# ACT and VectorE in a written order from the last head's output to the output projection, and the last row's scaling shared by both

## The chip, the core and the metric

The kernel runs on one core of one Trainium2 chip. A core has five engines with queues of their own: TensorE (PE, with its weight loads PEld), VectorE (DVE), ScalarE (ACT), GpSimd (POOL) and SyncE (SP), which here only issues transfers. Each takes its own instructions in order and waits on semaphores for the others. The metric is the device time of one execution in microseconds (us), the median of the runs.

## The reference

```python
h = rms_norm(x, norm_mix_g); u = h @ w_in            # 1024 tokens x 1024 -> 3328 columns
u_pool, q_raw, f_raw, i_raw, g_raw = split(u)        # 256 + 4 x 768 columns
y_pool = pool_mixer(u_pool)                          # trailing means over 2/4/8/16, a map per group
y_hgrn = hgrn2_mixer(q_raw, f_raw, i_raw, g_raw)     # 6 heads, state 128x128, chunkwise;
                                                     # per-head RMSNorm, swish gate on the output
x = x + concat([y_pool, y_hgrn]) @ w_out
x = x + square(relu(rms_norm(x) @ w_up)) @ w_down    # 4096 hidden channels
return rms_norm(x, final_norm_g)
```

All arrays are float32 and batch and depth are 1.

## The kernel before

**Products.** Every float32 operand of a large product is split into a rounded part `hi` and a remainder `lo`: `split` (L119) writes `hi` with an ACT cast (L121) and `lo` with a DVE subtraction that reads `hi` (L122). `mm3` (L124) then does three matmuls, hi*hi (L127), hi*lo (L128) and lo*hi (L129). A product with a weight block can so begin when the block's `whi` is there, and its third matmul needs `wlo` as well.

**The mixing stage** (the first 370 us) is a loop over six heads `hd` (L721). For each head the chain `hgrn` (L393) runs in stages named near, middle, far, keys, updates and output; beside it the generator `beside(hd)` (L603) makes the dense products that the next head needs (`q`, the forget input `f`, the gate `g`, for two heads the values `v` or the pooling input `u`). Between the stages PE takes as many steps of that dense work as the table `LAGS` says; one step is one k-tile, three matmuls. `load_w` (L159) brings a weight block from HBM into one of two `raw` buffers and splits it into a ring of four `whi` and four `wlo` buffers. A dense product `dense_T` (L346) sums eight steps into a PSUM bank, and DVE scales the bank into its tile (L355). `q` and `g` go through a sigmoid on ACT (L361) and a product on DVE (L362), `f` through three ACT operations (L367 to L369). For each head `hgrn` begins with DVE products (`d0`, `d1`, L398 to L401), `deepen` (L526) multiplies `q`, `k` and the decays level by level, and ACT copies pairs of blocks (`kq`, L410 and L411) for PE. The stage updates carries the state over seven chunks on DVE (`st`, L502 and L504). The stage output forms `po` on PE (L513 and L515), takes its squares on ACT (L518), the scale with DVE and POOL (`rstd_of`, L131), and the scaled output `on` on DVE (L520). `mixed` (L537) transposes `on` on PE (`pto`) and gates it into the `mix` tile (L544), one head later.

**The handover.** After the last head the eight `mix` tiles are split into `mT` (`mix_split`, L748), four blocks of the left half of `w_out` are loaded and split (`wo`), and PE computes the first two row tiles `ps_o` with k-tiles in the order of `MIX_ORDER` (2, 3, 4, 5, 6, 0, 1, 7). The transposes of the last head stand behind the first three k-tiles.

**What sets the order.** PE's order is written out through the whole mixing stage (`tc.manual_schedule` with PE alone, L720). The order of DVE, ACT and POOL there is the scheduler's: it may put an instruction ahead of what stands before it in the text. DVE and ACT are in a written order in the prologue, in the first group of the MLP (L989) and in the last two products.

**The end.** The last row tile's right half is computed in two pieces of 256 columns (L1237). Their sums of squares are taken on ACT (L1128), POOL makes the row scale (L1143), then DVE scales the left 512 columns (L1147, sent by SP) and ACT the right 512 (L1151, sent from ACT's own queue).

## Time and profile before

| what | value |
| --- | --- |
| three runs | 1071.29 to 1071.64 us, median 1071.42 us |
| the profiled execution | 1071.58 us, of which the span from first to last instruction is 1069.8 us |
| mean granted TensorE clock | 0.999 |
| PE busy | 1060.4 us (99%) |
| DVE busy | 741.7 us (69%) |
| ACT busy | 447.7 us (42%) |
| POOL busy | 77.3 us (7%) |

A row of the timeline gives start, duration, engine, line, operation, output and input, and in brackets how long the engine stood idle before and what ended that. A row of windows gives busy time and instruction count of PE, PEld, DVE, ACT and POOL in a stretch, then the granted clock, the DMA share and GB/s. The span's start is 0. Matmuls overlap: one lasts 0.39 us in the rows, while in a dense stretch the next starts some 0.23 us after it.

### The profile page before, as it was taken

How to read it: one execution, taken by the hardware profiler on the slowest of the kernel's cores; microseconds unless marked ns; L12 is line 12 of the kernel's file. 1: busy time of each engine (PE TensorE's matmuls, PEld its weight loads, DVE VectorE, ACT ScalarE, POOL GpSimd, SP SyncE). 2: the span in 40 equal slices, each digit the busy share in tenths (PEclk: the TensorE clock that was granted, in tenths of full speed). 3: DMA queues.
4: the chain of work that ended last, by engine and by line, in shares of the span. 5: the costliest groups of instructions: out<-in, count | busy, mean ns of one | idle time of the engine just before them, and what ended most of it. 6: DMA issues, size and time to landing. Idle time of an engine off the chain costs nothing.

```text
span 1069.8 us, 14595 instructions
## 1 busy us (share of the span) xinstructions
PE 1060.4 (99%) x5930; PEld 889.6 (83%) x5930; DVE 741.7 (69%) x928; ACT 447.7 (42%) x722; POOL 77.3 (7%) x126
## 2 busy tenths in 40 slices
PE   9999999999999999999999999999999999999997
PEld 8988889988888788888888888888888888888886
DVE  5377676166587924798856865876979878777775
ACT  5856545344444723463223223323435242423334
POOL 0001000001010111101101100100100000000001
PEclk9999999999999999999999999999999999999999
DMA  9521011031001633135435534428983344253104
GB/s 315 169 60 55 17 30 40 3 97 41 21 1 41 202 134 117 70 108 177 167 109 189 185 101 156 177 98 318 389 335 119 114 162 170 105 204 150 40 1 157
DMA packets 70515, 137.56 MB, mean 129 GB/s; under 512 B 5040, under 2 KB 44080, under 8 KB 66864
## 3 DMA queue, kind: packets, MB, share of 16 engines
q1 hardware_dynamic: 59808, 100.98, 27.8%
q0 software_dynamic: 9344, 33.56, 8.0%
q10 hardware_dynamic: 1296, 2.10, 0.5%
q8 instruction: 46, 0.75, 0.3%
q14 instruction: 21, 0.17, 0.1%
HBM read 98.87 MB, written 37.75 MB: 128 GB/s over the span
## 4 chain that ended last, share of the span: by engine, by line
PE 95%; DVE 3%; DMA 0%; issue 0%; POOL 0%; ACT 0%; SPq 0%; ACTq 0%; POOLq 0%
PE ps_ua L128 5%; PE ps_ua L127 5%; PE ps_ua L129 5%; PE ps_dx L129 5%; PE ps_dx L127 5%; PE ps_dx L128 5%; PE ps_v L283 3%; PE ps_dy L129 3%; PE ps_uc L128 3%; PE ps_dy L127 3%; PE ps_uc L127 3%; PE ps_uc L129 3%; PE ps_dy L128 3%; PE ps_o L129 2%; PE ps_o L128 2%; PE ps_o L127 2%
## 5 line engine op out<-in xcount | busy, mean ns | idle before, releaser
L121 ACT CAST wdop<-raw_wd 128x2048 fp32r<-128x2048 f32 x28 | 53.5, 1912 | 154.3 <-PE ps_dy L129 50.2
L127 PE MATMUL ps_ua<-h2op,whi_wu 128*128 128x512 f32 x256 | 99.7, 389 | 0.0
L129 PE MATMUL ps_ua<-h2op,wlo_wu 128*128 128x512 f32 x256 | 99.6, 389 | 0.0
L128 PE MATMUL ps_ua<-h2op,whi_wu 128*128 128x512 f32 x256 | 99.6, 389 | 0.0
L127 PE MATMUL ps_dx<-wdop,hop 128*128 128x512 f32 x252 | 98.0, 389 | 0.0
L128 PE MATMUL ps_dx<-wdop,hop 128*128 128x512 f32 x252 | 98.0, 389 | 0.0
L129 PE MATMUL ps_dx<-wdop,hop 128*128 128x512 f32 x252 | 98.0, 389 | 0.0
L122 DVE TENSOR_TENSOR wdop<-raw_wd,wdop 128x2048 fp32r<-128x2048 f32 x28 | 64.1, 2289 | 27.9 <-ACT wdop L121 27.9
L121 ACT CAST hop<-hraw 128x2048 fp32r<-128x2048 f32 x28 | 53.4, 1909 | 33.6 <-DMA hraw<-hid 21.0
L122 DVE TENSOR_TENSOR hop<-hraw,hop 128x2048 fp32r<-128x2048 f32 x28 | 63.9, 2283 | 2.2 <-ACT hop L121 2.2
L121 ACT CAST whi_wu<-wsum 128x1024 fp32r<-128x1024 f32 x22 | 23.2, 1053 | 93.6 <-DVE wsum L795 38.7
L122 DVE TENSOR_TENSOR wlo_wu<-raw_wu,whi_wu 128x1024 fp32r<-128x1024 f32 x23 | 28.0, 1221 | 47.6 <-ACT whi_wu L121 47.6
L798 DVE TENSOR_TENSOR x<-ps_dx,x 128x512 f32<-128x512 f32 x64 | 43.9, 687 | 18.7 <-PE ps_dx L129 18.7
L127 PEld LDWEIGHTS ps_ua<-h2op,whi_wu 128*128 128x128 f32 x256 | 48.1, 188 | 10.0
L129 PEld LDWEIGHTS ps_ua<-h2op,wlo_wu 128*128 128x128 f32 x256 | 48.0, 188 | 10.0
L128 PEld LDWEIGHTS ps_ua<-h2op,whi_wu 128*128 128x128 f32 x256 | 48.1, 188 | 9.9
L128 PEld LDWEIGHTS ps_dx<-wdop,hop 128*128 128x128 f32 x252 | 47.3, 188 | 9.9
L129 PEld LDWEIGHTS ps_dx<-wdop,hop 128*128 128x128 f32 x252 | 47.3, 188 | 9.8
L127 PEld LDWEIGHTS ps_dx<-wdop,hop 128*128 128x128 f32 x252 | 47.3, 188 | 9.8
L1031 POOL DMA_DIRECT2D hid<-hid x56 | 29.8, 532 | 283.6 <-DVE hid L1028 216.5
L127 PE MATMUL ps_uc<-h2op,whi_wu 128*128 128x512 f32 x128 | 49.8, 389 | 0.0
L128 PE MATMUL ps_uc<-h2op,whi_wu 128*128 128x512 f32 x128 | 49.8, 389 | 0.0
(280 smaller groups left out, 2706.4 us busy)
## 6 DMA issues: line engine op xcount, KB each, us to landing
hid<-hid POOLq DMA_DIRECT2D x56, 512.0 KB, 3.2
hraw<-hid SPq DMA_DIRECT2D x28, 1024.0 KB, 4.8
raw_wu<-in_w_up_dram SPq DMA_DIRECT2D x32, 512.0 KB, 3.8
raw_wd<-in_w_down_dram SPq DMA_DIRECT2D x16, 1024.0 KB, 7.1
xt<-in_x_t_dram SPq DMA_DIRECT2D x16, 256.0 KB, 5.4
xn<-in_x_dram SPq DMA_DIRECT2D x8, 512.0 KB, 7.9
x<-x_mid SPq DMA_DIRECT2D x8, 512.0 KB, 5.4
raw_q<-in_w_in_dram SPq DMA_DIRECT2D x6, 512.0 KB, 3.9
```

The lines of the kernel that those rows point to most:

```text
L121: act.copy(hi, src)
L122: dve.tensor_tensor(out=lo, in0=src, in1=hi.bitcast(F32), op=ALU.subtract)
L127: pe.matmul(ps, lh, rh, start=start, stop=False, skip_group_check=goes_on)
L128: pe.matmul(ps, lh, rl, start=False, stop=False, skip_group_check=goes_on)
L129: pe.matmul(ps, ll, rh, start=False, stop=stop, skip_group_check=goes_on)
L283: pe.matmul(banks[i][:, :VC], hT[h][part][:, j, i * P:(i + 1) * P], w[:, b, :], start=j == 0 and part == 0 and w is wh, stop=j == KT - 1 a ...
L798: dve.tensor_tensor(out=out_, in0=a, in1=b, op=ALU.add)
L1031: nc.gpsimd.dma_start(store[n][:, at, :], t)
```

## The change

Four things are edited. The stage output of `hgrn` is cut in two: both `po` tiles with their squares and scales come first, and a new stage "rows" with lag 0 holds both `on` products. From the last head's stage output to the second half of the `mix` splits, DVE and ACT are put into a written order (`in_order`), and the loads of `w_out` and the splits of `mix` are placed between the steps of that order. `pool_input` allocates its split tiles ahead of the gate weights. In the last row tile the second piece's squares move from ACT to DVE, the weighting with `gf` is done for its right half before the scale is known, and the scaling is shared as 704 columns on DVE and 320 on ACT.

```diff
@@ -30,9 +30,9 @@
 FILL = 160
 
 
-STAGES = ("near", "middle", "far", "keys", "updates", "output")
+STAGES = ("near", "middle", "far", "keys", "updates", "output", "rows")
 LAGS = {48: (5, 14, 8, 4, 1, 9), 64: (6, 19, 10, 4, 1, 10), 96: (6, 19, 10, 5, 2, 14)}
-LAGS = {steps: dict(zip(STAGES, lags)) for steps, lags in LAGS.items()}
+LAGS = {steps: dict(zip(STAGES, (*lags, 0))) for steps, lags in LAGS.items()}
 FIRST_LAG = 9
 WARM_UP = 8
 MIX_ORDER = (2, 3, 4, 5, 6, 0, 1, 7)
@@ -505,7 +505,7 @@
                         out=st[:, nxt, :], in0=st[:, i, :], scalar=t_m[:, i:i + 1], in1=u, op0=ALU.mult, op1=ALU.add,
                     )
             yield "output"
-            on = ha.tile([P, NT, P], F32, tag="Kn", name=f"on_{hd}", bufs=1)
+            pos = []
             for b in range(2):
                 po = misc_ps(f"po_{hd}_{b}")
                 for c in range(4):
@@ -516,7 +516,10 @@
                 ss = small.tile([P, 4], F32, tag="sso", name=f"sso_{hd}_{b}")
                 for c in range(4):
                     act.activation(junk[:, :P], po[:, c * P:(c + 1) * P], AF.Square, accum_out=ss[:, c:c + 1])
-                r = rstd_of(ss, 4, P, small, f"o_{hd}_{b}")
+                pos.append((po, rstd_of(ss, 4, P, small, f"o_{hd}_{b}")))
+            yield "rows"
+            on = ha.tile([P, NT, P], F32, tag="Kn", name=f"on_{hd}", bufs=1)
+            for b, (po, r) in enumerate(pos):
                 dve.tensor_tensor(
                     out=on[:, 4 * b:4 * b + 4, :], in0=po.rearrange("p (c t) -> p c t", c=4),
                     in1=r[:, :, None].to_broadcast([P, 4, P]), op=ALU.mult,
@@ -555,6 +558,7 @@
             u = ha.tile([P, S], F32, tag="GQ"[kt], name=f"u_{kt}", bufs=1 + kt)
             w = col_tile(kt * P, f"pool{kt}")
 
+            parts = [wring["split"][0].tile([P, S], F32R, tag=f"w{part}", name=f"w{part}_win_{kt}") for part in ("hi", "lo")]
             ready_w["g"] = gate_weights(NH - 2 + kt)
             for h in range(2):
                 yield from dense_T(by_chunk(u, h), w, h, f"pool{kt}")
@@ -573,7 +577,6 @@
                     out=wins[0][pr, :], in0=w[pr, :], scalar=pconst[pr, kt, PAD:], in1=u[pr, :],
                     op0=ALU.mult, op1=ALU.subtract,
                 )
-            parts = [wring["split"][0].tile([P, S], F32R, tag=f"w{part}", name=f"w{part}_win_{kt}") for part in ("hi", "lo")]
             for h in range(2):
                 cs = slice(h * HALF, (h + 1) * HALF)
                 split(parts[0][:, cs], parts[1][:, cs], wins[0][:, cs])
@@ -719,6 +722,22 @@
             pr = slice(e * 64, (e + 1) * 64)
             split(*(w[pr, :, pr] for w in pws), pw[pr])
 
+
+        ws, mT = [None] * (KT // 2), []
+
+        def left_rows_of(j):
+            src = w_out[0][j * P:(j + 2) * P, :512].rearrange("(j p) c -> p j c", p=P)
+            ws[j // 2] = load_w(src, [2, 512], f"wo_0_{j // 2}")
+
+        def mix_operand(h):
+            mT.append(tuple(big.tile([P, KT, 512], F32R, tag="big", name=f"mT_{part}{h}") for part in ("hi", "lo")))
+
+        def mix_split(h, j):
+            split(mT[h][0][:, j, :], mT[h][1][:, j, :], mix[j][:, h * 512:(h + 1) * 512])
+
+
+        in_order = tc.manual_schedule(engines={mybir.EngineType.DVE, mybir.EngineType.Activation})
+
         with tc.manual_schedule(engines={mybir.EngineType.PE}):
             for hd in range(NH):
                 work = beside(hd)
@@ -727,27 +746,24 @@
                     chain = hgrn(hd, *heads[hd], vts[hd])
                     stage = next(chain)
                 while stage:
+                    if hd == NH - 1 and stage == "output":
+                        in_order.__enter__()
                     for _ in range(lags[stage] + (FIRST_LAG if hd == 0 and stage == "near" else 0)):
                         next(work, None)
                     if stage == "middle" and hd:
                         mixed(hd - 1, on, gates[hd - 1])
+                    if hd == NH - 1 and stage == "rows":
+                        mix_operand(0)
+                        left_rows_of(MIX_ORDER[0])
+                        for j in MIX_ORDER[:3]:
+                            mix_split(0, j)
+                        left_rows_of(MIX_ORDER[2])
                     try:
                         stage = next(chain)
                     except StopIteration as end:
                         on, stage = end.value, None
                 finish(work)
 
-        def row_block(src, r0, n, c0, name):
-            return load_w(src[r0 * P:(r0 + n) * P, c0:c0 + 512].rearrange("(j p) c -> p j c", p=P), [n, 512], name)
-
-        ws = [None] * (KT // 2)
-        for j in MIX_ORDER[:-1:2]:
-            ws[j // 2] = row_block(w_out[0], j // 2 * 2, 2, 0, f"wo_0_{j // 2}")
-        mT = big_pair("mT")
-
-        def mix_split(h, j):
-            split(mT[h][0][:, j, :], mT[h][1][:, j, :], mix[j][:, h * 512:(h + 1) * 512])
-
         for pool_ in (psm, pss, psd):
             pool_.release()
         psb = ctx.enter_context(tc.tile_pool(name="psb", bufs=8, space=bass.MemoryType.PSUM, reuse_waits="tile"))
@@ -769,14 +785,20 @@
 
         with tc.manual_schedule(engines={mybir.EngineType.PE}):
             first_rows = {i: bank(f"ps_o_0_{i}") for i in range(2)}
-            for j in MIX_ORDER[:-1]:
+            products_out(first_rows, left_weight, MIX_ORDER[:3])
+            left_rows_of(MIX_ORDER[4])
+            for j in MIX_ORDER[3:5]:
                 mix_split(0, j)
-            products_out(first_rows, left_weight, MIX_ORDER[:3])
+            left_rows_of(MIX_ORDER[5])
+            for j in MIX_ORDER[5:7]:
+                mix_split(0, j)
             mixed(NH - 1, on, gates[NH - 1], bank)
             mix_split(0, MIX_ORDER[-1])
             products_out(first_rows, left_weight, MIX_ORDER[3:])
-        for j in MIX_ORDER:
-            mix_split(1, j)
+            mix_operand(1)
+            for j in MIX_ORDER:
+                mix_split(1, j)
+        in_order.__exit__(None, None, None)
     mixp.release()
 
     big2 = ctx.enter_context(tc.tile_pool(name="big2", bufs=3, side="right", reuse_waits="tile"))
@@ -1147,6 +1169,17 @@
             dve.scalar_tensor_tensor(out=ys[i][:, :512], in0=xs[i][:, :512], scalar=r, in1=gf[:, :512], op0=ALU.mult, op1=ALU.mult)
             nc.sync.dma_start(out[0, i * P:(i + 1) * P, :512], ys[i][:, :512])
 
+        def last_rows(i, r):
+
+            y, n = ys[i], 704
+            dve.tensor_scalar(y[:, :n], y[:, :n], r, None, op0=ALU.mult)
+            nc.sync.dma_start(out[0, i * P:(i + 1) * P, :n], y[:, :n])
+            act.mul(y[:, n:], y[:, n:], r)
+            act.dma_start(out[0, i * P:(i + 1) * P, n:], y[:, n:])
+
+        def weighted(i, cs):
+            dve.tensor_tensor(out=ys[i][:, cs], in0=xs[i][:, cs], in1=gf[:, cs], op=ALU.mult)
+
         def right_rows(i, r):
             act.mul(ys[i][:, 512:], ys[i][:, 512:], r)
             act.dma_start(out[0, i * P:(i + 1) * P, 512:], ys[i][:, 512:])
@@ -1245,19 +1278,29 @@
                     if cs.stop == 256:
 
                         ss = squares(i, cs)
+                        weighted(i, cs)
                         left_rows(*ready)
                         both = small.tile([P, 1], F32, tag="part", name=f"ss_{i}_left", bufs=8)
                         dve.tensor_scalar(both, ss, 1.0 / D, sss[i], op0=ALU.mult, op1=ALU.add)
                         sss[i] = both
                         continue
+                    if cs.start == 256:
+
+                        ss = small.tile([P, 1], F32, tag="ss3", name=f"ss3_{i}_last", bufs=16)
+                        x_ = xs[i][:, cs]
+                        dve.scalar_tensor_tensor(
+                            out=junk[:, cs], in0=x_, scalar=1.0, in1=x_, op0=ALU.mult, op1=ALU.mult, accum_out=ss
+                        )
+                        r = row_scale(i, ss)
+                        weighted(i, cs)
+                        right_rows(*ready)
+                        last_rows(i, r)
+                        continue
                     ss = squares(i, cs)
                     if ready:
-                        if cs.start % 512 == 0:
-                            left_rows(*ready)
+                        left_rows(*ready)
                         right_rows(*ready)
                     ready = i, row_scale(i, ss)
-            left_rows(*ready)
-            right_rows(*ready)
 
 
 # ---- launch: one core; inputs and outputs as the reference has them ----
```

PE's order and POOL's are the same before and after. DVE's and ACT's differ from the first head on. Three places follow. In names `whi_q` and `wlo_q` are the split query weights, `kq` the pair copies, `sso` the sums of squares of `po`, and the numbers are buffers.

ACT, from the end of head 0 to the pair copies of head 1. Before:

```order
L361 ACTIVATE ps_g_0_938<-g_931 128x512
L410 COPY kq_2_1098<-Q_702 128x512
L411 COPY kq_2_1098<-K_704 128x2x128x2
L121 CAST whi_q_1530<-raw_q_1528 128x1024
L361 ACTIVATE ps_g_1_1006<-g_931 128x512
L518 ACTIVATE junk,sso_0_1059<-po_0_1051 128x128 x4
L518 ACTIVATE junk,sso_1_1078<-po_1_1069 128x128 x4
L410 COPY kq_4_1156<-Q_702 128x512
```

Now:

```order
L361 ACTIVATE ps_g_0_940<-g_933 128x512
L361 ACTIVATE ps_g_1_1008<-g_933 128x512
L518 ACTIVATE junk,sso_0_1060<-po_0_1052 128x128 x4
L518 ACTIVATE junk,sso_1_1078<-po_1_1069 128x128 x4
L410 COPY kq_2_1100<-Q_704 128x512
L411 COPY kq_2_1100<-K_706 128x2x128x2
L121 CAST whi_q_1108<-raw_q_1106 128x1024
L410 COPY kq_4_1158<-Q_704 128x512
```

The query weights cast here before, `whi_q_1530`, are those of head 3, which PE reads a whole turn later. Now the cast is `whi_q_1108`, those of head 2, which PE's order reads directly behind `po_1`; it stands behind the eight squares and behind both copies `kq_2`.

DVE at the same place. Before:

```order
L122 TENSOR_TENSOR wlo_q_1531<-raw_q_1528,whi_q_1530 128x1024
L362 TENSOR_TENSOR g_931<-ps_g_1_1006,g_931 128x512
L534 TENSOR_TENSOR dec_1093<-dec_1093 128x128
L134 TENSOR_SCALAR ms_o_0_1064<-sso_0_1059 128x4
L534 TENSOR_TENSOR dec_1093<-dec_1093 128x64
L520 TENSOR_TENSOR on_1050<-po_0_1051,rstd_o_0_1066 128x512
L534 TENSOR_TENSOR dec_1093<-dec_1093 128x32
L534 TENSOR_TENSOR dec_1093<-dec_1093 128x16
L534 TENSOR_TENSOR dec_1093<-dec_1093 128x8
L134 TENSOR_SCALAR ms_o_1_1083<-sso_1_1078 128x4
L520 TENSOR_TENSOR on_1050<-po_1_1069,rstd_o_1_1085 128x512
```

Now:

```order
L134 TENSOR_SCALAR ms_o_0_1065<-sso_0_1060 128x4
L134 TENSOR_SCALAR ms_o_1_1083<-sso_1_1078 128x4
L523 TENSOR_TENSOR on_1087<-po_0_1052,rstd_o_0_1067 128x512
L523 TENSOR_TENSOR on_1087<-po_1_1069,rstd_o_1_1085 128x512
L398 TENSOR_TENSOR d_1_1090<-Q_704,K_706 128x1024
L399 TENSOR_TENSOR Q_704<-Q_704,F_705 128x1024
L401 TENSOR_TENSOR d_1_1093<-Q_704,K_706 128x512
L533 TENSOR_TENSOR Q_704<-Q_704,F_705 128x2x256
L534 TENSOR_TENSOR K_706<-K_706,F_705 128x2x256
L537 TENSOR_TENSOR dec_1095<-F_705 128x512
L122 TENSOR_TENSOR wlo_q_1109<-raw_q_1106,whi_q_1108 128x1024
L439 COPY_PREDICATED within<-dmask,sc_near 128x256
```

Between the scaled outputs `on` and head 2's remainder `wlo_q_1109` there stand now the six first products of head 1. Before, that remainder stood ahead of head 0's own first products, and those of head 1 were past when `on` came.

ACT behind the last head's gate. Before:

```order
L121 CAST mT_hi_3533<-mix_1227 128x512
L121 CAST mT_hi_3533<-mix_1675 128x512
L121 CAST mT_hi_3533<-mix_2286 128x512
L121 CAST mT_hi_3533<-mix_2750 128x512
L121 CAST mT_hi_3533<-mix_3206 128x512
L518 ACTIVATE junk,sso_0_3442<-po_0_3434 128x128
L121 CAST mT_hi_3533<-mix_3170 128x512
L121 CAST whi_win_3394<-winK_3066 128x512 x2
L361 ACTIVATE ps_g_0_3401<-g_3400 128x512
L518 ACTIVATE junk,sso_0_3442<-po_0_3434 128x128
L121 CAST whi_wo_1_3511<-raw_wo_1_3509 128x1024
```

Now:

```order
L121 CAST whi_win_3192<-winK_3068 128x512 x2
L361 ACTIVATE ps_g_0_3403<-g_3402 128x512
L518 ACTIVATE junk,sso_0_3443<-po_0_3435 128x128 x4
L518 ACTIVATE junk,sso_1_3461<-po_1_3452 128x128 x4
L121 CAST whi_wo_1_3474<-raw_wo_1_3472 128x1024
L121 CAST mT_hi_3470<-mix_1229 128x512
L121 CAST mT_hi_3470<-mix_1677 128x512
L121 CAST mT_hi_3470<-mix_2288 128x512
L121 CAST whi_wo_2_3486<-raw_wo_2_3484 128x1024
L592 ACTIVATE mix_3502<-psp_0_3503,pscale 128x256 x2
L592 ACTIVATE mix_3502<-psp_1_3509,pscale 128x256 x2
L361 ACTIVATE ps_g_1_3431<-g_3402 128x512
```

The five casts of `mix` tiles that stood ahead of the squares stand now behind all of them, and behind the first block of `w_out`.

## The prediction

> **What bounds the kernel now.** First the page's busy times and the chain of waits, then the waits by engine, then the windows around the handover.
>
> ```profile
> PE 1060.4 (99%) x5930; PEld 889.6 (83%) x5930; DVE 741.7 (69%) x928; ACT 447.7 (42%) x722; POOL 77.3 (7%) x126
> PE 95%; DVE 3%; DMA 0%; issue 0%; POOL 0%; ACT 0%; SPq 0%; ACTq 0%; POOLq 0%
> ...
> PE ps_o L129 <- DVE mT_lo L122: 0.9, 2, 0.5
> ...
> 340.00:372.00 32.00, 31.09 (x157) 25.50 (x156) 29.91 (x51) 18.89 (x45) 2.32 (x2) 1.00 0.42 140
> 372.00:1060.00 688.00, 688.00 (x3069) 570.11 (x3068) 501.44 (x497) 245.08 (x271) 47.47 (x86) 1.00 0.43 156
> ```
>
> PE is busy 99% of the span and carries 95% of the chain. It waits for another engine almost nowhere behind the prologue: twice, 0.9 us in all, for `mT_lo` in the handover (340 to 372 us, the only stretch of these with PE idle: 32.0 less 31.09). From 372 us on it never stops, and takes 688 us for 3069 recorded matmuls, 0.224 us each. PE's order is written and the same in both kernels, so the time changes only where PE waits. What can be won is 0.9 us and the end; what can be lost is every place where DVE and ACT come later than PE now needs them.
>
> **The change, part by part.** The orders above show that not only the handover moves. Through all six heads the splits of the weight blocks stand now directly ahead of their use, where before they ran a turn earlier. Each such place becomes a chain that starts with PE's own last result, and PE stands behind it. I work them out with PE's present times as the clock, 0.03 us at each change of engine, and the start-to-start times of the rows where one engine goes on.
>
> Query weights behind a head's output:
>
> ```profile
> 65.02 1.23 DVE L398 TENSOR_TENSOR d<-Q,K 128x1024 f32<-128x1024 f32 x1 [0.73 <-ACT K L369]
> 66.36 1.23 DVE L399 TENSOR_TENSOR Q<-Q,F 128x1024 f32<-128x1024 f32 x1
> 67.61 0.69 DVE L401 TENSOR_TENSOR d<-Q,K 128x512 f32<-128x512 f32 x1
> 69.42 0.68 DVE L531 TENSOR_TENSOR K<-K,F 128x512 f32<-128x512 f32 x1
> 70.20 0.68 ACT L411 COPY kq<-K 128x512 f32<-128x512 f32 x1
> ...
> 100.84 1.05 ACT L121 CAST whi_q<-raw_q 128x1024 fp32r<-128x1024 f32 x1 [2.80 <-PE ps_g L128]
> 102.46 1.22 DVE L122 TENSOR_TENSOR wlo_q<-raw_q,whi_q 128x1024 fp32r<-128x1024 f32 x1
> 104.00 0.39 PE L515 MATMUL po<-st,Q 128*128 128x128 f32 x2
> 104.14 0.48 PE L127 MATMUL ps_q<-hT_hi,whi_q 128*128 128x512 f32 x1
> 105.86 0.19 ACT L518 ACTIVATION_READ_ACCUMULATOR junk<-po 128x1 f32 x1
> 106.80 0.17 DVE L134 TENSOR_SCALAR ms_o<-sso 128x4 f32<-128x4 f32 x1
> 108.09 0.69 DVE L520 TENSOR_TENSOR on<-po,rstd_o 128x512 f32<-128x512 f32 x1 [1.13 <-POOL rstd_o L136]
> ```
>
> `po` ends at 104.39 (104.00 + 0.39) and today `ps_q` starts at once, since `wlo_q` (102.46) was early. Now the weights come behind `on` and the next head's products. The squares end 1.66 us after `po` (105.86 + 0.19). The scale follows 0.07 us later, `on` 1.29 us after it (106.80 to 108.09), and the first product 0.61 us on: 3.63 us. From the start of `d` to that of K's product are 4.40 us (65.02 to 69.42), of which 0.6 us go to an unrelated instruction that is gone, while a wait of 0.1 us comes in: 3.9 us, and 0.69 us to its end. Then the copy (next start 0.6 us on), the cast 1.05 us, the remainder 1.22 us: 7.55 us after `d` began, 11.2 us after `po`. PE's third matmul would have started 0.3 us after `po`. The stop is **10.9 us** after head 0. After heads 1 and 3 gate products (21 or 42 matmuls, 4.7 or 9.4 us) still follow `po`, and `d` waits in DVE's queue behind that gate: scale 0.69, sigmoid 0.60, product 0.6 us, with changes 1.98 us after the gate's last matmul, then 7.55 us, less 0.3: **9.25 us each**. Sum 29.4 us.
>
> Gate or pooling weights behind the forget product:
>
> ```profile
> 86.29 0.39 PE L127 MATMUL ps_g<-hT_hi,whi_g 128*128 128x512 f32 x1
> 86.49 0.69 DVE L355 TENSOR_TENSOR K<-ps_f,rms_row 128x512 f32<-128x512 f32 x1 [0.82 <-PE ps_f L129]
> 88.33 0.63 ACT L367 ACTIVATE F<-K 128x512 f32<-128x512 f32 x1
> 88.99 0.63 ACT L368 ACTIVATE K<-K 128x512 f32<-128x512 f32 x1
> 89.66 0.72 ACT L369 ACTIVATE K<-K,om 128x512 f32<-128x512 f32 x1
> ...
> 97.22 2.26 DVE L504 SCALAR_TENSOR_TENSOR st<-st,dec,pu 128x128 f32<-128x128 f32 x6
> 131.53 1.72 PE L496 MATMUL pu<-V,kn 128*128 128x128 f32 x14
> 133.01 0.48 PE L127 MATMUL ps_g<-hT_hi,whi_g 128*128 128x512 f32 x1
> ```
>
> Today `ps_g` starts at 86.29 while `ps_f` still drains. Now the cast is behind the three ACT operations on `ps_f`: DVE 0.72 us, then 1.96 us of ACT starts (0.66, 0.67, 0.63), cast 1.05, remainder 1.22, with changes 5.05 us after `ps_f`, less 0.3: **4.75 us** at head 3. At head 0 DVE reaches the forget product 1.5 us late, since the middle stage's three selects and four deepening products now stand ahead of it and wait there for ACT's `kq` copies: **6.25 us**. At heads 1 and 4 DVE also has the state chain ahead: PE's `pu` ends 133.25, six steps 2.26 us, then the same 5 us and more, against a need at 133.5: **7.0 us each**. Sum 25.0 us. Queued behind the waiting cast are the copies of `scores` and `kn`, still in time.
>
> Weights behind a sigmoid, and the places where a head's tiles come from elsewhere:
>
> ```profile
> 77.31 0.60 ACT L361 ACTIVATE ps_q<-Q 128x512 f32<-128x512 f32 x1
> ...
> 208.90 0.89 ACT L339 ACTIVATE V<-ps_v,rms_col 128x128 f32<-128x128 f32 x3 [3.27 <-PE ps_v L129]
> raw_v<-in_w_in_dram SPq DMA_DIRECT2D x4, 384.0 KB, 3.2
> ...
> 310.26 0.69 DVE L355 TENSOR_TENSOR u<-ps_pool,rms_row 128x512 f32<-128x512 f32 x1 [0.34 <-PE ps_pool L129]
> 310.99 1.23 DVE L566 TENSOR_TENSOR win<-u 128x1023 f32<-128x1023 f32 x1
> 313.98 2.60 DVE L572 SCALAR_TENSOR_TENSOR win<-win,pconst,u 64x1024 f32<-64x1024 f32 x2
> 313.56 0.86 PE L391 MATMUL sc_near<-d,ones 128*32 128x256 f32 x16
> 317.55 1.29 DVE L122 TENSOR_TENSOR wlo_win<-win,whi_win 128x512 fp32r<-128x512 f32 x2
> ```
>
> For `f` at heads 1, 2, 3 and 4 and `q` at head 3 the cast follows the second sigmoid: 0.72 + 0.6 + 1.05 + 1.22 us, less 0.3, is 3.3 us; heads 2 and 3 (`q`) are 0.3 us later. With the pooling weights of head 5, which stand behind four scalings of `mix` instead: **20.4 us**. The values (four blocks in two raw buffers): blocks 3 and 4 load only when 1 and 2 are split, 3.2 us and their issue, then a cast and a remainder in about 0.9 us each: **6.8 us**. The gate behind them waits for three scalings (0.89 us) and both `kq` copies: **4.0 us**. At head 5 the near stage needs `d`: today at 313.56. Now DVE first finishes the pooling windows (310.26 to 316.58), their remainders (to 318.4), and then the products and copies, 5.3 us more, so that the pair products start 13.5 us after the pooling product instead of 4.0: **9.5 us**.
>
> The handover. The same walk through the third pair of orders: `wlo_win` is 0.75 us late, because all window sums stand behind the whole state chain. The squares of `po` stand behind the gate's sigmoid, so the first block of `w_out` is cast at 357.7, `mT_lo` is ready at 360.6 instead of before 356.5, and the sixth k-tile waits for a sigmoid that itself waits behind `on`. The first two row tiles end 4.25 us later still, with the old 0.9 us inside: **5.0 us** together. Copies and casts beyond that have ten microseconds of cover in the next row tiles.
>
> Sum of the stops: 29.4 + 25.0 + 20.4 + 6.8 + 4.0 + 9.5 + 5.0 = **100.1 us**.
>
> PE's clock. A stopped PE may come back slower:
>
> ```profile
> 1.18 3.59 PE L230 MATMUL warm<-junk 128*128 128x512 bf16 x8 [1.18 <-DVE junk L228]
> 5.87 0.38 PE L283 MATMUL ps_v<-whi_v,hT_hi 128*128 128x384 f32 x1
> ...
> 1062.00:1063.00 1.00, 0.68 (x6) 0.48 (x4) 0.80 (x2) 0.51 (x2) 0.17 (x1) 1.00 0.91 334
> 1067.00:1068.00 1.00, 0.00 (x0) 0.00 (x0) 0.00 (x0) 0.00 (x0) 0.00 (x0) 0.75 0.95 350
> 1068.00:1069.80 1.80, 0.00 (x0) 0.00 (x0) 0.00 (x0) 0.00 (x0) 0.00 (x0) 0.50 0.02 5
> ```
>
> The first eight matmuls of 512 columns take 0.45 us each (3.59 / 8), twice the 0.224 us of the dense stretch, and the short spacing begins near 5.87 us, 4.7 us after the first matmul. At the end the last matmul is over at 1062.7 and the granted clock is 0.5 from about 1067.5: 4.8 us of rest. So a stop beyond 4.8 us may cost 4.7 us at half speed, 2.35 us. By the sums above seven rests are longer: 10.0, 8.3, 8.3, 8.1, 5.9, 5.9 and 5.3 us. I take the four long ones whole and three at half: **12.9 us**, bounds 0 and 42 us (all 18 stops).
>
> The Trainium skill (TensorE: Matmul & The Clock Gate, Part 1: The HAM clock gate) has the array fall to half rate after an idle window of about 3.4 us and come back after about as much work. By its figures, as an estimate, the nine stops over 3.4 us would cost up to 1.7 us each, 15 us, and the time would be 1186 us. It is the rule that speaks most against this change.
>
> The end:
>
> ```profile
> 1064.05 0.21 DVE L1141 TENSOR_SCALAR ms_n<-ss,ss_left 128x1 f32<-128x1 f32 x1 [0.64 <-ACT junk L1128]
> 1064.92 0.75 DVE L1147 SCALAR_TENSOR_TENSOR y<-x,rstd_n,gf 128x512 f32<-128x512 f32 x1 [0.66 <-POOL rstd_n L1143]
> ```
>
> The squares of the last 256 columns move to DVE, which spares ACT's way (0.64 us of DVE's idle) but adds 0.4 us of DVE; the last scaling covers 704 columns at 0.75 us per 512 or less. I take **-0.4 us**, bounds -0.8 and +0.3.
>
> The profiled execution took 1071.58 us, 0.16 us above the median, which changes nothing here. 1071.6 + 100.1 + 12.9 - 0.4 = **1184 us**.
>
> **The rivals.** *The clock stays.* The rests are too short or the first matmuls of each chain, hi*hi and hi*lo, which start 1.2 us ahead of the third, break them: 1171 us. For it speaks that 4.8 us is one observation; against, four rests beyond 8 us.
>
> *Every stop slows the clock.* If the gate goes by a share of busy time, stops 15 us apart keep it down: 18 x 2.35 = 42 us, 1213 us. Against it: the one fall of the clock that the records show came only after 4.8 us of rest.
>
> *The loads fall behind as well.* A raw buffer is free only after the late split, so each load starts later; if six of them end behind their need by 4 us (one load's 3.2 us and its issue), 1208 us. Against it: between two splits into one buffer lie at least two dense products of 24 matmuls, 10.8 us.
>
> *Not slower.* The splits come late in the list only, DVE and ACT having time to spare (58% and 31% idle): then PE meets no new wait, the old 0.9 us go and the end gains, 1070.3 us. That would need `wlo_q` within 0.3 us after `po`. It decides for it only if the chains above do not depend on PE's last result; the rows say they do.
>
> **How the numbers follow.** The forecast has 0.66, its own range 1171 to 1198 us (10% of the stops, four to seven slow starts). The clock that stays 0.15, every stop slow 0.08, loads 0.07, not slower 0.04. The range of 8 in 10 is 1163 to 1212 us. About 0.2% (2 us) is what a measurement can tell from no change: faster 0.01, same 0.03, slower 0.96.
>
> **What would show it.** In the waits of PE, `ps_q`, `ps_g`, `ps_f` and `ps_pool` waiting for ACT's `whi` and DVE's `wlo`, three stops of 9 to 11 us after `po` or the gate, `ps_v` waiting for the third block, `sc_near` once for DVE. The stage up to `ps_o` lasts to about 469 us instead of 356, and from there to the end nothing changes. The granted clock is below 1.00 after the long stops. I am wrong if PE's waits stay under 10 us in all, if they sum to much more or less than 100 us, or if the stretch after 470 us differs.

## The result, and the profile after

The changed kernel took 1200.92 us (median, 1199.31 to 1202.79) against 1071.29 us for the kernel before: a ratio of 1.1209, 95% interval 1.1193 to 1.1226. 1184 us were predicted, with a range of 8 in 10 of 1163 to 1212. The time lies inside that range, but 3 us above the 1171 to 1198 us that the forecast gave to its own sum. The sign, the places and the mechanism were right; two sizes were too small, the stops by some 5 us and the slow clock by some 11.

The page's busy times, the granted clock in the 40 slices, and the head of the chain of waits, of the changed kernel:

```profile
PE 1103.7 (92%) x5930; PEld 911.3 (76%) x5930; DVE 749.5 (63%) x932; ACT 446.4 (37%) x720; POOL 74.4 (6%) x126
...
PEclk9998887898989879999999999999999999999999
...
PE 86%; DVE 9%; ACT 4%; issue 1%; POOL 0%; POOLq 0%; DVEq 0%; ACTq 0%
```

PE has the same 5930 matmuls. DVE and ACT, which had 3% and 0% of the chain before, have 9% and 4%: ten points of 1197.5 us, some 120 us, have come onto engines that hid behind PE. The granted clock is below nine tenths in nine of the slices 4 to 15 and nowhere behind them. The mean granted clock is 0.953 instead of 0.999.

PE's waits, where behind the warm-up one line stood before:

```profile
PE ps_q L127 <- ACT whi_q L121: 29.5, 4, 9.8
PE ps_g L127 <- ACT whi_g L121: 18.2, 4, 6.0
PE ps_f L127 <- ACT whi_f L121: 11.1, 4, 3.2
PE ps_pool L127 <- ACT whi_pool L121: 8.4, 2, 6.0
PE sc_near L391 <- DVE d L398: 6.1, 1, 6.1
PE ps_v L127 <- ACT whi_v L121: 3.6, 1, 3.6
PE ps_o L127 <- ACT mT_hi L121: 2.2, 1, 2.2
PE sc_near L419 <- ACT kq L411: 1.4, 1, 1.4
...
PE ps_q L129 <- DVE wlo_q L122: 0.5, 1, 0.5
```

The first eight rows are 80.5 us of waiting for a cast (`whi`) or for a tile of the head, the names that the prediction gave; all rows of the view behind the warm-up make 85 us. Rows of the timeline show single stops, each with PE's idle time in brackets:

```profile
91.56 0.79 PE L127 MATMUL ps_g<-hT_hi,whi_g 128*128 128x512 f32 x1 [5.45 <-ACT whi_g L121]
121.42 0.79 PE L127 MATMUL ps_q<-hT_hi,whi_q 128*128 128x512 f32 x1 [9.81 <-ACT whi_q L121]
189.72 0.79 PE L127 MATMUL ps_q<-hT_hi,whi_q 128*128 128x512 f32 x1 [8.24 <-ACT whi_q L121]
355.08 0.79 PE L127 MATMUL ps_q<-hT_hi,whi_q 128*128 128x512 f32 x1 [8.23 <-ACT whi_q L121]
481.88 0.49 PE L127 MATMUL ps_o<-whi_wo,mT_hi 128*128 128x512 f32 x1 [2.22 <-ACT mT_hi L121]
```

And what stands ahead of the longest of them, the one of 9.81 us, on DVE and ACT (an excerpt of their timelines):

```profile
114.60 0.69 DVE L523 TENSOR_TENSOR on<-po,rstd_o 128x512 f32<-128x512 f32 x1 [0.54 <-POOL rstd_o L136]
115.21 1.22 DVE L398 TENSOR_TENSOR d<-Q,K 128x1024 f32<-128x1024 f32 x1
...
119.77 0.66 ACT L411 COPY kq<-K 128x512 f32<-128x512 f32 x1
120.33 1.04 ACT L121 CAST whi_q<-raw_q 128x1024 fp32r<-128x1024 f32 x1
...
121.40 1.23 DVE L122 TENSOR_TENSOR wlo_q<-raw_q,whi_q 128x1024 fp32r<-128x1024 f32 x1 [1.07 <-ACT whi_q L121]
```

That is the forecast chain in its order: `on`, `d`, the next head's first products, the copies `kq` that read them, and only then the weights' cast and remainder.

Windows: the handover's 32 us and the 688 us behind it, as quoted of before, moved by 125.8 us; then three stretches of 3.41 us around the first stop (the number ahead of the last two is the granted clock):

```profile
465.80:497.80 32.00, 28.33 (x131) 22.18 (x130) 26.46 (x41) 17.50 (x42) 2.01 (x2) 0.95 0.32 106
497.80:1185.80 688.00, 688.00 (x3068) 570.18 (x3067) 502.57 (x499) 245.76 (x272) 46.92 (x85) 1.00 0.43 157
...
84.76:88.18 3.42, 1.35 (x6) 0.75 (x5) 2.35 (x6) 2.19 (x5) 0.00 (x0) 1.00 0.00 0
88.18:91.59 3.41, 0.03 (x1) 0.03 (x1) 0.37 (x2) 2.91 (x4) 0.77 (x1) 0.50 0.00 0
91.59:95.00 3.41, 3.37 (x7) 2.26 (x8) 1.17 (x1) 0.00 (x0) 0.00 (x0) 0.50 0.26 74
```

From 497.8 us on the kernel is the old one: PE never idle, 688.0 us, clock 1.00. All the loss lies ahead of it: the last matmul starts 127.9 us later than before (1190.27 against 1062.40 us), and so does one at 496.40 us (368.45 before). Behind the stop of 5.45 us PE works a whole stretch at clock 0.50. The granted clock falls in this way behind each of the seventeen stops of 2.2 us and more, or still within the long ones, for one to three stretches of 3.41 us.

### The profile page after: what moved, and what is told of

It reads as the page before. It is cut to its first block, busy times and chain, and to the rows that moved or that the text cites. A ratio compares the mean times of both kernels' runs of the same rounds, so it can differ in the third digit from the quotient of the medians.

```text
span 1197.5 us, 14593 instructions
## 1 busy us (share of the span) xinstructions
PE 1103.7 (92%) x5930; PEld 911.3 (76%) x5930; DVE 749.5 (63%) x932; ACT 446.4 (37%) x720; POOL 74.4 (6%) x126
## 4 chain that ended last, share of the span: by engine, by line
PE 86%; DVE 9%; ACT 4%; issue 1%; POOL 0%; POOLq 0%; DVEq 0%; ACTq 0%
PE ps_ua L127 5%; PE ps_ua L129 5%; PE ps_ua L128 5%; PE ps_dx L128 5%; PE ps_dx L129 5%; PE ps_dx L127 5%; PE ps_v L283 3%; PE ps_dy L128 2%; PE ps_uc L127 2%; PE ps_uc L129 2%; PE ps_dy L129 2%; PE ps_dy L127 2%; PE ps_uc L128 2%; PE ps_o L129 2%; PE ps_o L127 2%; PE ps_o L128 2%
## 5 line engine op out<-in xcount | busy, mean ns | idle before, releaser
L127 PE MATMUL ps_ua<-h2op,whi_wu 128*128 128x512 f32 x256 | 99.7, 389 | 0.0
L129 PE MATMUL ps_ua<-h2op,wlo_wu 128*128 128x512 f32 x256 | 99.7, 389 | 0.0
L129 PE MATMUL ps_dx<-wdop,hop 128*128 128x512 f32 x252 | 98.1, 389 | 0.0
L127 PE MATMUL ps_dx<-wdop,hop 128*128 128x512 f32 x252 | 98.1, 389 | 0.0
L127 PE MATMUL ps_q<-hT_hi,whi_q 128*128 128x512 f32 x96 | 42.0, 437 | 29.5 <-ACT whi_q L121 29.5
L121 ACT CAST hop<-hraw 128x2048 fp32r<-128x2048 f32 x28 | 53.3, 1908 | 34.3 <-DMA hraw<-hid 22.8
L127 PE MATMUL ps_g<-hT_hi,whi_g 128*128 128x512 f32 x96 | 43.3, 451 | 18.2 <-ACT whi_g L121 18.2
L129 PEld LDWEIGHTS ps_ua<-h2op,wlo_wu 128*128 128x128 f32 x256 | 48.1, 188 | 10.0
L127 PEld LDWEIGHTS ps_ua<-h2op,whi_wu 128*128 128x128 f32 x256 | 48.1, 188 | 9.9
L127 PEld LDWEIGHTS ps_dx<-wdop,hop 128*128 128x128 f32 x252 | 47.3, 188 | 9.9
L129 PEld LDWEIGHTS ps_dx<-wdop,hop 128*128 128x128 f32 x252 | 47.3, 188 | 9.7
L127 PE MATMUL ps_f<-hT_hi,whi_f 128*128 128x512 f32 x96 | 41.2, 429 | 11.1 <-ACT whi_f L121 11.1
```

Of the source, the lines that this page charges most:

```text
L121: act.copy(hi, src)
L127: pe.matmul(ps, lh, rh, start=start, stop=False, skip_group_check=goes_on)
L129: pe.matmul(ps, ll, rh, start=False, stop=stop, skip_group_check=goes_on)
```

## The experiments

### Where the written order begins

The diff enters the order at the last head's output, yet all six heads lost their old order. The kernel before makes and enters such an order in adjacent lines (L989, L990); the change makes the object ahead of the head loop (L739) and enters it inside (L750). The first experiment moves the making to the entering line, and ends the order at the end of the loop, with a second one for the block behind it (excerpts, here and below, with the engines' names shortened):

```diff
-        in_order = tc.manual_schedule(engines={DVE, Activation})
         with tc.manual_schedule(engines={PE}):
             for hd in range(NH):
...
                     if hd == NH - 1 and stage == "output":
+                        in_order = tc.manual_schedule(engines={DVE, Activation})
                         in_order.__enter__()
...
                 finish(work)
+            in_order.__exit__(None, None, None)
...
-        with tc.manual_schedule(engines={PE}):
+        with tc.manual_schedule(engines={PE, DVE, Activation}):
             first_rows = ...
...
-        in_order.__exit__(None, None, None)
```

> The changed kernel, but the object of the written order is made where it is entered (last head, stage output) and closed at the end of the head loop; the second block of the handover is put in order by a region of its own. Theory A (the order holds from where the object is made, ahead of the head loop, and only the order inside the six heads costs): the six heads go back to the old order, the handover keeps the stops that the changed kernel shows there (0.5 us for psp, 3.1 us for ps_o, 2.4 us of slow clock behind it, less the old 0.9 us), the end gains 0.4: 1071.3 + 0.5 + 3.1 + 2.4 - 0.9 - 0.4 = 1076 us at most, 1071 if the stops there came from lateness brought along from the heads; ratio to before 1.000 to 1.005. Rival B (a written order at the handover is itself what costs, through buffers that come free late): near 1200 us, 1.12.

Measured: 1073.87 us, ratio 1.0022, interval 1.0012 to 1.0031. Of the 130 us some 2 are left. PE's waits at the handover:

```profile
PE ps_o L129 <- DVE mT_lo L122: 1.6, 1, 1.6
...
PE ps_o L127 <- ACT mT_hi L121: 0.8, 1, 0.8
PE ps_o L128 <- DVE wlo_wo L122: 0.2, 1, 0.2
```

1.6 + 0.8 + 0.2 is 2.6 us against the old 0.9: 1.7 of the 2.3 us. No stop is left in the heads, and `wlo_q` stands at 103.27 us, ahead of `on`:

```profile
103.27 1.22 DVE L122 TENSOR_TENSOR wlo_q<-raw_q,whi_q 128x1024 fp32r<-128x1024 f32 x1
...
106.49 0.69 DVE L523 TENSOR_TENSOR on<-po,rstd_o 128x512 f32<-128x512 f32 x1 [0.94 <-POOL rstd_o L136]
```

The order holds from the line where the object is made, not from the one where it is entered. Lists of instructions, from programs that were built and not run, say so too: a kernel whose head loop is declared in order for PE, DVE and ACT as a whole has the changed kernel's order of DVE and ACT instruction by instruction, but for the last gate's sigmoid and one DVE instruction at the loop's very end, while moving the entering line to the next stage changes nothing.

Next, the order in the second block alone (`first_rows` up to the second half of the splits), and none at all, for which the line with the three engines stays as it was, with PE alone:

```diff
-        in_order = tc.manual_schedule(engines={DVE, Activation})
...
-                        in_order.__enter__()
...
-        with tc.manual_schedule(engines={PE}):
+        with tc.manual_schedule(engines={PE, DVE, Activation}):
             first_rows = ...
...
-        in_order.__exit__(None, None, None)
```

> The changed kernel with DVE and ACT in order in the second block of the handover alone (first two row tiles, last head's transposes, second half of the splits). Theory A: PE has no new stop in the heads; 1070.0 to 1072.5 us, ratio 0.999 to 1.001, with the old wait of 0.9 us for mT_lo kept or gone. Rival B: near 1200 us.

> The changed kernel without any written order for DVE and ACT in the handover; the stage rows, the moved allocation, the moved loads and the new end stay. Theory A: 1070.3 to 1071.5 us, ratio 0.999 to 1.000 (the end's -0.4 us). Rival C (the cut of the output stage, the moved loads or the allocation cost the time, not the order): 1195 to 1201 us.

Measured: 1070.13 us, ratio 0.9987 (0.9978 to 0.9996), with the second block in order; 1071.50 us, ratio 1.0002 (0.9993 to 1.0011), without any. The cut of the output stage, the moved loads and the moved allocation cost nothing that can be seen. An order in the second block is worth about 1.4 us, and this kernel beats both. Waits of PE without an order:

```profile
PE ps_o L127 <- ACT mT_hi L121: 0.5, 1, 0.5
PE ps_o L129 <- DVE mT_lo L122: 0.5, 1, 0.5
```

With it there is no wait for `ps_o` at all in that view.

### The end alone

The kernel before with the edits of `last_rows`, `weighted` and the last loop alone.

> The kernel before with the edit of the last row alone (second piece's squares on DVE, weighting ahead of the scale, 704 columns on DVE and 320 on ACT). By the prediction's term -0.4 us, 1070.9 us, ratio 0.9996, bounds -0.8 and +0.3 us. Rival: the 0.4 us of squares and the longer DVE scaling eat the gain, 1071.3 us or more.

Measured: 1071.69 us, ratio 1.0001 (0.9992 to 1.0010): too small to be told. The traces give the step. Before, the last matmul, DVE's scale input, and DVE's last scaling (1064.05 and 1064.92 us in the prediction's rows):

```profile
1062.40 0.28 PE L129 MATMUL ps_last<-wdop,hop 128*128 128x256 f32 x1
```

With the new end:

```profile
1062.85 0.28 PE L129 MATMUL ps_last<-wdop,hop 128*128 128x256 f32 x1
...
1063.93 0.43 DVE L1269 SCALAR_TENSOR_TENSOR junk<-x 128x256 bf16<-128x256 f32 x1
...
1064.40 0.21 DVE L1141 TENSOR_SCALAR ms_n<-ss_last,ss_left 128x1 f32<-128x1 f32 x1
...
1065.38 0.58 DVE L1153 TENSOR_SCALAR y<-y,rstd_n 128x704 f32<-128x704 f32 x1 [0.44 <-POOL rstd_n L1143]
```

The scale's input comes 1.55 us after the start of the last matmul instead of 1.65, the scaling 2.53 instead of 2.52; the squares on DVE take nearly the time that the way over ACT took. Only the scaling is shorter, 0.58 instead of 0.75 us. From the start of the last matmul to the end of the span (1069.8 and 1070.1 us) it is 7.25 instead of 7.40 us: 0.15 us gained where 0.4 us was forecast.

### Waiting and slow clock told apart

PE is given idle products of the identity to do while it waits, in the bank that the next product starts anew. The first of two such kernels fills the waits of the heads up to 0.8 us before the block comes, the second to some 0.2 us, and the handover's too:

```diff
+        def fill(ps, name):
+            for _ in range(FILLING.get(name, 0)):
+                pe.matmul(ps[:, :P], ident, ident, start=True, stop=True)
...
             ps = dense_ps(f"ps_{name}_{h}")
+            if h == 0:
+                fill(ps, name)
```

> The changed kernel with 6 to 36 idle products of the 128x128 identity on PE ahead of each of the 16 waiting products in the heads (about 0.245 us each, so that they end some 0.8 us before the waited block comes); they write the bank that the product behind them starts anew, so the result is the same. Theory A (the 127.7 us are 85 us of waiting and some 43 us of matmuls at half the clock behind each rest): the rests go, the waiting stays, the granted clock stays near 1.00, and the 0.75 us that a remainder comes after a first pair at full rate show again (16 x 0.75 = 12 us): 1071.3 + 85 + 12 - 0.5 = 1168 us, between 1156 and 1172. Rival (the lower clock has another reason than the rests, or costs nothing beside the waits): 1195 to 1201 us.

> As the filled kernel, with more idle products (22 for the first gate, 41 for the second query, and so on, about 0.233 us each), so that a rest of some 0.2 us is left ahead of the block, and with a few in the three later stops (near of head 5, the first row tile). The filled kernel still had six half-rate periods of 3.4 us. Theory A (the changed kernel's 127.9 us are 85 us for whi and the like, 19 us for remainders and the rest behind the first matmul, and 24 us of slow clock): the last half-rate periods go too, and what is left are the stops alone: 1071.3 + 104 = 1175 us, 1173 to 1180. Rival (the slow clock was worth 15 us only, the rest is waiting that no filling moves): 1183 to 1188 us, as the filled kernel.

Measured: 1185.90 us (ratio 1.1069, 1.1050 to 1.1087) for the first, outside both expected ranges: six half-rate stretches were left, and the stops are longer than the 97 us put down for them. 1178.09 us (1.0992, 1.0974 to 1.1010) for the second, inside its range of 1173 to 1180, with a mean clock of 0.996 and one such stretch. From PE's last own matmul to the waited one its stops are as long as in the changed kernel, to 0.05 us in sixteen places and 0.15 us in one: they are chains from PE's own result. Waits of PE in the second:

```profile
PE ps_v L127 <- ACT whi_v L121: 2.5, 2, 2.1
PE ps_q L127 <- ACT whi_q L121: 2.3, 4, 0.7
PE ps_q L129 <- DVE wlo_q L122: 2.1, 4, 0.5
```

Here the remainder is waited for 0.5 us every time, where the changed kernel showed it once in four for `ps_q`: there the first two matmuls mostly ran at half rate and covered it. So of the 129.6 us 1200.9 - 1178.1 = 22.8 us are slow clock. The one slow stretch left in the second kernel, behind a stop of 2.06 us for the values, costs some 1.6 us more, so it is about 24 us of slow clock and 105 us of stops.

### The same order, with the blocks asked for earlier

The change's own order, but each block is loaded and split in the text when the second half of the product ahead of it begins (`next_of`), instead of at its own product. Of the values only the first two blocks can come early. One place of the edit:

```diff
                 for h in range(2):
+                    if h:
+                        next_of(f"q{hd + 1}")
                     yield from gated(q, wq, h, f"q_{hd + 1}")
```

> The changed kernel, its written order kept, but each weight block is loaded and split in the text half a dense product earlier (when the second half of the product ahead of it begins). Theory A (only the place of the splits in the order costs): the stops of q, f, g and pool weights go (29.5 + 18.2 + 11.1 + 8.4 us, but for the 3.0 us of the gate behind the values), and the slow clock behind them; left are near of head 5 (8.4 us), the handover (3.6 us), the values and their gate (5 us) and four slow starts (10 us): 1097 us, between 1085 and 1110. Rival (an order by hand costs in any case: the splits now stand ahead of the products of the next head, and PE waits for those instead): 1130 us or more.

Measured: 1120.28 us, ratio 1.0451 (1.0435 to 1.0466), 10 us above the range of theory A and 10 us under the rival's. The long stops for weights are gone and 80 of 130 us with them, but new ones came:

```profile
PE sc_near L395 <- DVE d L402: 7.5, 2, 6.1
PE sc_near L423 <- ACT kq L415: 6.0, 4, 1.6
PE sc_near L395 <- DVE d L405: 4.2, 4, 1.3
PE ptk L492 <- DVE K L538: 2.5, 2, 1.3
```

The stages of the head wait 17.7 us for `d` and `kq`, 9.3 more than in the changed kernel (6.1 + 1.4 + 0.9), and 2.5 us for `K`. Both theories hold a part: the place of the splits was most of it, but this text order, which serves the weights, keeps the heads' own tiles back. In the kernel before, in the scheduler's order, PE waits for neither.

### One queue in order, the other free

The order for DVE alone, and in the other kernel for ACT alone (`{Activation}` in the same place):

```diff
-in_order = tc.manual_schedule(engines={DVE, Activation})
+in_order = tc.manual_schedule(engines={DVE})
```

> The changed kernel with its written order for DVE alone (from the same place); ACT's order is the scheduler's. The casts may run ahead again, the remainders may not. Theory A (either queue keeps a block back, since PE needs both parts): the stops move from the first matmul of a product to its third and are 1.1 to 1.7 us shorter, since cast and copies no longer stand in the chain: 1071.3 + 104 - 16 x 1.4 + 18 = 1171 us, 1155 to 1185. Rival (only the casts matter): within 10 us of before.

> The changed kernel with its written order for ACT alone. Theory A: the casts are as late as in the changed kernel wherever ACT itself waits for PE's last result; what DVE's own queue added (the state chain, the windows) goes: 1175 to 1200 us, with the waits for whi in first place. Rival (only the order of DVE matters): within 10 us of before.

Measured, one execution each and so without an interval: 1170.73 us and 1174.03 us. Waits of PE with DVE in order:

```profile
PE ps_q L129 <- DVE wlo_q L122: 29.0, 4, 9.4
```

and with ACT in order:

```profile
PE ps_q L127 <- ACT whi_q L121: 13.1, 4, 3.7
```

Either queue alone keeps a block back: with DVE in order the stop moves from the first matmul (L127) to the third (L129), with ACT it stays at the first. With DVE alone the expected 1171 us were met, but partly by luck: all of PE's waits in that view, behind the warm-up, make some 70 us where 82 were expected, and the rest of the loss is some 29 us where 18 were put down for the clock. ACT alone came out 1 us under its range: without DVE's queue ahead of it the longest stop for `ps_q` is 3.7 us, not 9.8.

### Stops of known length

In the kernel before, in groups 1 to 7 of the MLP, one tiny product waits for a number of copies on ACT that begin with PE's last result:

```diff
                     banks[key] = up_banks(g, key)
+                    if n == 2 and g:
+                        for k in range(COPIES[g - 1]):
+                            act.copy(junk, junk if k else banks["a"][1])
+                        pe.matmul(banks[key][0][:, :P], junk[:, :P], junk[:, :P], start=True, stop=True)
```

> The kernel before; in groups 1 to 7 of the MLP PE waits once for 1, 2, 3, 4, 5, 6 and 8 copies of 512 columns on ACT in a row that start with PE's own last result (rests of about 0.8, 1.3, 1.9, 2.4, 3.0, 3.6 and 4.8 us, some 18 us in all). Theory A (a rest of about 2.2 us is enough, as all stops of the changed kernel say): the granted clock falls behind the last four, 2.4 us each: 1071.3 + 18 + 10 = 1099 us. Theory B (the prediction's: a rest of 4.8 us): it falls behind the last at most, 1092 us. Theory C (it goes by the share of busy time over longer windows): a single rest does not lower it, 1089 us.

> The kernel before with seven equal stops in the MLP, one copy on ACT each, 2.15 us by the first stop of the run before, which did not lower the clock, while 2.87 us and more did. Theory A (the clock is set in free-running stretches of 3.41 us, by whether PE was busy for half of the one before; so the same rest lowers it or not by how the stretches cut it): some of the seven lower it and some don't; those that do are those that lie in one stretch with more than 1.7 us. Theory B (a threshold between 2.15 and 2.2 us of rest): none lowers it, 1071.3 + 15 = 1086 us. With n falls, 1086 + 2 n us.

Measured, one execution each: 1118.9 us and 1094.5 us. The stops of the first were longer than meant, 32.6 us in all, because ACT's first copy also waited for DVE. Some of them:

```profile
521.18 0.23 PE L1061 MATMUL ps_ub<-junk 128*128 128x128 bf16 x1 [2.15 <-ACT junk L1060]
562.46 0.23 PE L1061 MATMUL ps_ub<-junk 128*128 128x128 bf16 x1 [2.87 <-ACT junk L1060]
```

The clock fell behind every one but that of 2.15 us, so theories B and C of the first run are out. In the second run six stops of 2.10 to 2.27 us and one of 3.38 us cost 16.6 us of waiting, and it fell behind two: that of 3.38 and one of the six, the shortest of all. So theory A of the second holds in kind; the time is 4.5 us above its 1086 + 2 x 2. Stretches of 3.41 us in which PE was stopped for 2.23 and for 2.10 us, each with the stretch behind it:

```profile
557.72:561.13 3.41, 1.53 (x7) 0.94 (x5) 3.41 (x5) 1.33 (x2) 0.00 (x0) 1.00 0.00 0
561.13:564.54 3.41, 3.06 (x14) 2.56 (x15) 3.08 (x3) 0.30 (x1) 0.53 (x1) 1.00 0.52 166
598.68:602.09 3.41, 1.31 (x8) 0.77 (x6) 3.41 (x5) 1.63 (x2) 0.00 (x0) 1.00 0.05 11
602.09:605.50 3.41, 3.41 (x9) 2.67 (x9) 2.63 (x3) 0.00 (x0) 0.53 (x1) 0.50 0.62 209
```

The longer stop leaves PE busy for 1.53 us of its stretch and 0.35 us of it fall into the next; the clock stays, although more than theory A's 1.7 us of rest lie in one stretch. The shorter one lies in one stretch whole, leaves 1.31 us, and the next stretch is granted half. So no threshold on the rest explains both; the share of a stretch of a grid that runs on by itself does. All clock changes of one run lie on one grid of 3.41 us. The kernel with DVE alone in order has a stronger case: a stop of 3.23 us for `wlo_f` (292.88 to 296.12 us) is cut by the grid into stretches with 1.56 and 2.04 us busy, and the clock stays at 1.00.

## Why the prediction was right, and where it was off

**The bound and the mechanism** were right. PE's order is the bound, the splits stood directly ahead of their use through all six heads, and each became a chain from PE's last result. What the prediction took from the orders without a reason has one now: the order begins where its object is made.

**The terms of the stops** can be measured one by one in the second filled kernel: how much later than in the kernel before the same matmul of PE starts, behind a stop against ahead of it. For the first query block, the last matmul of `po` starts at 110.54 instead of 104.11 us and the ninth of the product behind it at 123.41 instead of 106.09: 17.32 less 6.43, 10.9 us.

| stops | forecast, us | measured, us |
| --- | --- | --- |
| query weights behind an output, three | 29.4 | 29.6 |
| gate and pooling weights, six (25.0 + 4.0 + 3.3) | 32.3 | 33.3 |
| behind a sigmoid, `f` four times and `q` once | 17.1 | 19.8 |
| values | 6.8 | 7.8 |
| near of head 5 | 9.5 | 9.5 |
| handover | 5.0 | 5.4 |
| sum | 100.1 | 105.4 |

The 1.6 us of that kernel's slow stretch are taken off the values. The first three terms name the same stops as the waits for `whi` in the changed kernel (9.81, 8.24 and 8.23 us for the query weights), with some 1.1 us more each: the remainder comes 0.9 us behind the cast, and the starts lie 0.2 us further apart than the idle time in brackets says. The values' stop is two, and the second, 2.1 us, does not show in the changed kernel's waits, where PE was still at half rate. So the sum was right to some 5 us, and half of the shortfall is the sigmoid's 2.7 us. The prediction's sign that PE's waits would sum to about 100 us did not come out as it stands: the view shows 85 us, since at half rate PE hardly waits for the remainders.

**The clock** is the step that failed: 12.9 us forecast, about 24 us measured. "A stop beyond 4.8 us may cost 4.7 us at half speed" was taken from the one rest at the end of the run; the known stops show that 2.10 us can be enough. The 4.8 us were not a threshold but the way to the grid's next edge: the stretch in which PE ends is busy for 2.02 us, and only the next is empty.

```profile
1060.66:1064.08 3.42, 2.02 (x17) 1.82 (x16) 2.33 (x7) 2.33 (x8) 0.54 (x1) 1.00 0.53 195
1064.08:1067.49 3.41, 0.00 (x0) 0.00 (x0) 0.94 (x2) 1.27 (x2) 0.54 (x1) 1.00 0.62 232
1067.49:1069.80 2.31, 0.00 (x0) 0.00 (x0) 0.00 (x0) 0.00 (x0) 0.00 (x0) 0.50 0.21 73
```

The rival "every stop slows the clock" had the right count (all stops), for the reason of a share of busy time, and by its 1213 us it was nearer to the result than the forecast. Its price was wrong, 2.35 us each: 24 us over seventeen stops is 1.4 us. A stretch at half rate costs up to 1.7 us of work, part of it lies under the rest itself (88.18 to 91.59 us above is idle and slow), and part covers the wait for the remainder, which would have come anyway. The two errors, 5 us of stops and 11 us of clock, go the same way; the result lies within 1163 to 1212 us because that range was wide enough for both.

The Trainium skill (TensorE: Matmul & The Clock Gate, Part 1: The HAM clock gate) has a free-running window of 3413 ns. The grid of 3.41 us agrees. It has the array fall after an idle window; the runs show a fall after a stretch that was 0.38 busy (1.31 of 3.41 us), so the nine stops over 3.4 us that the prediction counted by it, 15 us, were too few.

**The end**: -0.4 us forecast, about -0.15 us in the traces, not measurable in the time. **Behind 470 us nothing changes**: right, with 498 us in place of 470. The rival *clock stays* (1171 us) is near the second filled kernel's 1178, which is nearly what that case would have been. *Not slower* needed a chain that does not depend on PE; the rows show that it does. (Its idle shares are the wrong way round: by the page DVE is idle for 31% and ACT for 58%.) *Loads behind*: in the groups of instructions no cast of a head's query, forget or gate block stood idle for a transfer; one for the values did, 3.58 us, and that is in the forecast's term:

```profile
L121 ACT CAST whi_f<-raw_f 128x1024 fp32r<-128x1024 f32 x6 | 6.3, 1049 | 0.0
```

## What to carry to other kernels

Where a scheduler places what isn't written out, look at what a written region does to the instructions far from it: here the place where the region's object is made, one line ahead of a loop, cost 130 us, and the same order kept to its block gained 1.4. A stop of an engine that bounds the kernel is priced by its chain from that engine's last result, and these prices were good to some 5% in sum. Count a slow start too behind stops from some 2 us on, about 1.4 us each here; idle products in the wait took it away.

## What the runs showed of the hardware

In all runs the granted clock changes only on a grid of 3.41 us that runs on whatever PE does, and it goes by how busy PE was in the stretch before: behind 1.51 us and less it always fell to half, behind more than 1.9 us it never did. Between these both came. It stayed behind the 1.53 us of the equal stops, and in the changed kernel it fell behind 1.89 us, at the handover:

```profile
480.71:484.12 3.41, 1.89 (x6) 1.14 (x7) 2.78 (x4) 3.41 (x7) 1.01 (x1) 1.00 0.05 15
484.12:487.53 3.41, 3.41 (x10) 2.64 (x9) 3.18 (x5) 1.35 (x5) 0.00 (x0) 0.50 0.55 195
```

So the clock goes by something near the busy time of these rows, and not by that alone. From half rate it came back behind no stretch with less than 2.83 us busy, and stayed there behind some with up to 3.10 us (272.50 to 275.91 us in the changed kernel), so the slow stretches end only behind nearly unbroken work. At half rate 2.83 to 3.10 us hold the work of 1.4 to 1.55 us at full rate, which would fit a count of work and not of time; no run here tests that.
